# A hybrid decoder step: the query and the outer products of a sample step issued back to back, with one accumulator bank per head

## The chip, the cores and the metric

The kernel runs on one core of one Trainium2 chip. The metric is device time in microseconds for one execution. Three executions of the kernel before took 2542.88, 2548.21 and 2549.33 us (median 2548.21). One more execution was profiled; the rows below and in the prediction come from it.

## The reference, cut to what matters

One layer of a decoder is computed for a prompt of 512 tokens and for a batch of 8 decoding sequences of 4 tokens each (32 sample tokens), width 2048. A wide input projection gives queries, keys, values and gates of an mLSTM branch (4 heads of 512) and of a sliding-window attention branch (32 query heads, 4 key heads), and the gates of a merge; two projections, a merge, an output projection and a layer norm follow. The change lies in the mLSTM branch of the sample tokens. There each head of each sequence has a stored state, a 512 x 512 matrix C:

```python
num = jnp.einsum('bhts,bhsd->bhtd', s, v) + inter[..., None] * jnp.einsum('bhtk,bhkv->bhtv', q, C)
...
C_new = decay[..., None, None] * C + jnp.einsum('bhsk,bhsv->bhkv', w[..., None] * k, v)
```

For the samples there is one chunk of 4 tokens, so each of the 32 matrices (8 sequences x 4 heads, 1 MB each) is read once, queried (`q C`), updated by an outer product of keys and values, and written back.

## The kernel before, in words

**Input projection.** The core's time is mostly matmuls of split operands: a weight tile `raw` (128 x 1024) is cast to `wh` by ScalarE (line 198) and the rest `wl` is subtracted by VectorE (line 199), and three products are accumulated. In the stage of interest (`paired`, line 643) two column blocks of the weights form a pair, and seven *products* (`half_product`, line 602) make a pair. A product is 24 matmuls of 272 columns (16 at line 610, 8 at line 612) into a PSUM tile `bank`; a pair has three banks: products 0 and 3 write the first, 1 and 5 the second, 2, 4 and 6 the third. After each product `gather` (line 614) reads the bank, on ScalarE after products 0, 1 and 3 and on VectorE after 2, 4, 5 and 6 (lines 631, 635, 637, 639); after product 1 GpSimd also adds a piece (line 629). There are 72 pairs. The buffers of `bank` come from a pool of four in turn, so that one is spare.

**Work beside it.** Everything else of this stage is written as generators. After each product `tick` lets every live generator run to its next `yield`, so a `yield` is the distance of one product on TensorE. The order on TensorE is the order in which the code is written (`manual_schedule` for TensorE alone); the other engines' queues, SyncE's DMA queue among them, are ordered by a scheduler. `high_priority` pulls splits and gathers forward.

**Sample heads.** After the attention of the prompt and of the samples, `samples` (line 1131) runs `sample_head` (line 1068) for the four heads in turn. A head starts with `sample_prep`: small loads (`qs`, `ks`, `vs`, the normaliser), two yields, then a GpSimd copy `rep` of the keys into four parts (`four_parts`, line 972), two yields, and TensorE's products and transposes of it (lines 1000, 1001, 1005), and so on. Then come 8 *steps* (`s` = 0, 1: four of the eight sequences; `c` = 0 to 3: 128 of the 512 rows of C). Per step:

- the tile `ct` holds four blocks of C (1 MB, one load, two buffers); `qz` holds the queries, zero outside the sequence's own tokens (GpSimd memset and four copies, lines 1088 and 1091, two buffers);
- four yields; at the first the previous step's updated C is stored (`store`, two DMAs of 512 KB), at the third the next block is loaded (`load_C`), whose buffer must have been stored;
- the *query*: four matmuls with 32 output columns of the array each, side by side (line 1101), into a PSUM tile `sm`; ScalarE copies the result out (line 1105 or 1108) and GpSimd adds it to a sum in SBUF (line 1109, `r["sum"]`, which holds the buffer named `rep`);
- one yield;
- the *outer products*: four matmuls with 32 rows of the array each (line 1114) into four `sm` tiles, which VectorE folds into `ct` (line 1117, four of 128 x 512).

After the 8 steps `sample_finish` scales the sum, waits until the output gates of the head are computed (`gated`), and finishes the head. `sm` has four banks.

Of the kernel before, what the change touches and what calls it, by code (L numbers as in the profile page):

```python
# [15 lines left out]
F32 = mybir.dt.float32  # L16
F32R = mybir.dt.float32r
AF = mybir.ActivationFunctionType
ALU = mybir.AluOpType
# [60 lines left out]
def _build(tc, nc, i, o, es):  # L80
    PSUM = bass.MemoryType.PSUM
    ALL = slice(0, 128)

    def pool(stack, name, bufs, space=None, side=None):
        kw = {"space": space} if space is not None else {}
        if space is None:
            kw["side"] = side or "right"
            kw["reuse_waits"] = "tile"
        return stack.enter_context(tc.tile_pool(name=name, bufs=bufs, **kw))

    y_p, y_s, C_p, n_p, m_p, kb_p, vb_p, C_s, n_s, m_s, kb_s, vb_s = o
    V, A, G, PE = nc.vector, nc.scalar, nc.gpsimd, nc.tensor
# [7 lines left out]
    esP, psA = es.enter_context(ExitStack()), {}  # L100

    def open_psum(pairs):

        esP.close()
        psA["mm"] = pool(esP, "psP" if pairs else "psA", 4 if pairs else 2, PSUM)

    open_psum(False)
    dr = pool(es, "dr", 1, bass.MemoryType.DRAM)
# [3 lines left out]
    def nm(s):  # L112
        count[0] += 1
        return f"{s}_{count[0]}"

    def sm():
        return psB.tile([128, 512], F32, tag="sm", name=nm("sm"))
# [4 lines left out]
    def r32(ap):  # L122
        return ap.bitcast(F32)
# [830 lines left out]
    def st1(shape, tag, dt=F32, p="s1p"):  # L954
        return sp[p].tile(shape, dt, tag=tag, name=nm(tag))

    def w512():
        return sp["sw"].tile([128, 512], F32, tag="w", name=nm("w"))
# [10 lines left out]
    def four_parts(src):  # L969

        rep = st1([128, 4, 128], "rep")
        G.tensor_copy(by_part(rep[:]), src[:].rearrange("p c (b t) -> p (c b) t", t=NTS).unsqueeze(2)
                      .to_broadcast([128, 4 * NB, 4, NTS]))
        return rep
# [8 lines left out]
    def sample_prep(h, r):  # L983
        qs = st1([128, 4, NS], "qs", p="sw")
        ks_, vs = (st1([128, 4, NS], t_) for t_ in ("ks", "vs"))
        hc = slice(h * 4, h * 4 + 4)
        for t_, d_ in ((qs, d_q), (ks_, d_k), (vs, d_v)):
            nc.sync.dma_start(t_[:], d_[hc, :, SEQ:T].rearrange("c p t -> p c t"))
        nh_ = w512()
        nh = nh_[:8]  # L990
        nc.sync.dma_start(nh, i["state_mlstm_n"][:, h, :])
        yield
        yield
        rep = four_parts(ks_)
        yield
        yield

        pS, pb = sm(), sm()
        for c in range(4):
            PE.matmul(pS[:, 0:NS], rep[:, c], qs[:, c], start=(c == 0), stop=(c == 3))  # L1000
        PE.matmul(pb[:, 0:NS], cc[0:4, C_ID + h:C_ID + h + 1].to_broadcast([4, 128]), nM[:, SEQ:T],
                  start=True, stop=True)
        pk = sm()
        for c in range(4):
            PE.transpose(pk[:, c * 128:c * 128 + 128], rep[:, c], ident)
        ds, dl = st1([128, NS], "ds"), st1([128, NS], "dl")
        V.tensor_tensor(out=dl[:], in0=pb[:, 0:NS], in1=cc[:, C_SM:C_SM + NS], op=ALU.add)
        A.activation(dl[:], dl[:], AF.Exp, bias=colT1[:, 4, 0, h:h + 1])
        V.tensor_tensor(out=ds[:], in0=pS[:, 0:NS], in1=dl[:], op=ALU.mult)
        V.scalar_tensor_tensor(dl[:], pS[:, 0:NS], cc[:, C_R + 10:C_R + 11], dl[:], op0=ALU.mult, op1=ALU.mult)  # L1010
        Ph, Pst = st1([128, NS], "Ph", F32R), st1([128, NS], "Pst", F32R)
        A.copy(Ph[:], ds[:])
        V.scalar_tensor_tensor(Pst[:], r32(Ph[:]), cc[:, C_R + 11:C_R + 12], dl[:], op0=ALU.mult, op1=ALU.add)

        kA = st1([128, 512], "kA", F32R)
        rows_of_parts(kA, st1([128, 512], "Ab", F32R), pk, C_R + 11, (colW[:, 0, h:h + 1], colW[:, 1, h:h + 1]))
        repv = four_parts(vs)
        yield
        yield

        pvv = sm()
        for c in range(4):
            PE.transpose(pvv[:, c * 128:c * 128 + 128], repv[:, c], ident)
        V4 = st1([128, 512], "V4", F32R)
        rows_of_parts(V4, st1([128, 512], "Ab", F32R), pvv, C_R + 13, (1.0, cc[:, C_R + 12:C_R + 13]))

        pn = sm()
        for c in range(4):
            PE.transpose(pn[:, c * 8:c * 8 + 8], nh[:, c * 128:c * 128 + 128], ident[:8, :8])
        nT = st1([128, 4, NB], "nT")  # L1030
        V.tensor_copy(nT[:].rearrange("p c b -> p (c b)"), pn[:, 0:32])
        yield
        pq = sm()
        for c in range(4):
            PE.matmul(pq[:NS, 0:NB], qs[:, c], nT[:, c], start=(c == 0), stop=(c == 3))
        pd = sm()
        PE.matmul(pd[:NS, 0:2], Pst[:], ones_r[:], start=True, stop=True)
        pnn = sm()
        PE.matmul(pnn[:8, :], m8r[:], kA[:], start=True, stop=True)
        den = st1([32, 16], "den", p="sw")  # L1040
        V.scalar_tensor_tensor(den[:, 0:8], pq[:NS, 0:NB], colT2[0:32, 4, 1, h:h + 1], cc[0:32, C_M8:C_M8 + 8],
                               op0=ALU.mult, op1=ALU.mult, accum_out=den[:, 8:9])
        V.tensor_tensor(out=den[:, 9:10], in0=pd[:NS, 0:1], in1=den[:, 8:9], op=ALU.add)
        V.scalar_tensor_tensor(nh, nh, dcc[:, h:h + 1], pnn[:8, :], op0=ALU.mult, op1=ALU.add)
        nc.sync.dma_start(n_s[:, h, :], nh)
        r.update(kA=kA, V4=V4, Pst=Pst, den=den, qs=qs)
# [21 lines left out]
    def sample_head(h):  # L1068
        r = {}
        nxt = load_C(h, 0, 0)  # L1070
        yield from sample_prep(h, r)
        stores = []

        def store():

            with tc.issue_after(state["load"].ins):
                for dst, src in stores:
                    nc.sync.dma_start(dst, src)
            stores.clear()

        for s in range(2):
            Ab = st1([128, 512], "Ab", F32R)
            G.tensor_scalar(Ab[:], r32(r["kA"][:]), cc[:, C_R + 8 + s:C_R + 9 + s], None, op0=ALU.mult)
            for c in range(4):
                ct, more = nxt, (s, c) != (1, 3)

                qz = st1([128, 4, NS], "qz", p="sw")
                G.memset(qz[:], 0.0)
                for b in range(4):
                    t = (b * 2 + s) * NTS  # L1090
                    G.tensor_copy(qz[:, b, t:t + NTS], r["qs"][:, c, t:t + NTS])
                for j in range(4):
                    yield
                    if j == 0:
                        store()
                    elif j == 2 and more:
                        with tc.issue_after(state["load"].ins):
                            nxt = load_C(h, s + (c == 3), (c + 1) % 4)
                pC = sm()
                for b in range(4):  # L1100
                    PE.matmul(pC[b * 32:b * 32 + 32, :], qz[:, b], ct[:, b], start=True, stop=True,  # L1101
                              tile_position=(0, b * 32))
                if (s, c) == (0, 0):
                    r["sum"] = st1([128, 512], "rep")
                    A.copy(r["sum"][:], pC[:])
                else:
                    some = w512()
                    A.copy(some[:], pC[:])
                    G.tensor_tensor(out=r["sum"][:], in0=r["sum"][:], in1=some[:], op=ALU.add)
                yield  # L1110
                pus = [sm() for _ in range(4)]
                for b in range(4):
                    rows = slice(b * 32, b * 32 + 32)
                    PE.matmul(pus[b][:], Ab[rows, c * 128:c * 128 + 128], r["V4"][rows], start=True, stop=True,  # L1114
                              tile_position=(b * 32, 0))
                for b in range(4):
                    V.scalar_tensor_tensor(ct[:, b], ct[:, b], dcb[:, h, b * 2 + s:b * 2 + s + 1], pus[b][:],
                                           op0=ALU.mult, op1=ALU.add)
                    if b % 2:
                        stores.append((C_s[s + b * 2 - 2:s + b * 2 + 1:2, h, c * 128:c * 128 + 128, :].rearrange("b p v -> p b v"),  # L1120
                                       ct[:, b - 1:b + 1]))
        yield
        store()
        while h not in gated:
            yield
        yield from sample_finish(h, r)
# [458 lines left out]
    for g in range(G3):  # L1585
        ct = 16 - G3 + g
# [48 lines left out]
```

## Time and profile before

| | |
|---|---|
| three runs | 2542.88, 2548.21, 2549.33 us |
| profiled execution, its time | 2543.75 us |
| its span (first to last instruction) | 2541.9 us |
| TensorE matmul busy | 2509.8 us (99%) |
| VectorE, ScalarE, GpSimd busy | 1709.8, 1195.5, 377.4 us |
| mean granted TensorE clock | 0.994 |
| sample steps on TensorE | from 1085.4 to 1762.8 us |

In the timeline a row is a run of instructions of one line: start, time from the first to the last end, engine, line, operation, output and inputs, the tile of the array used (rows*columns) and the shape, how many. A matmul's own duration (some 290 ns) is longer than its distance to the next (about 125 ns), since matmuls overlap; the distance between starts is what counts. The four matmuls of a query appear as 8 records.

### The profile page before, as it was taken

The numbers are of one execution on the slowest core, as the hardware profiler recorded it, in microseconds if no ns is written. First come the engines' busy times: TensorE is split into PE (matmuls) and PEld (weight loads), VectorE is DVE, ScalarE is ACT, GpSimd is POOL, SyncE is SP. The second block draws the span as 40 slices with busy tenths as digits, with TensorE's granted clock in tenths as the row PEclk, the third lists the DMA queues.
The fourth block names the chain that finished last, engine by engine and source line by source line (L and its number), as shares of the span: only waits on it lengthen the run. The fifth ranks groups of instructions, "written<-read, shape, count | busy, mean of one in ns | idle before, by whom it ended". The sixth has DMA issues, their size and how long they took to land.

```text
span 2541.9 us, 48994 instructions
## 1 busy us (share of the span) xinstructions
PE 2509.8 (99%) x19995; PEld 2443.5 (96%) x19995; DVE 1709.8 (67%) x2506; ACT 1195.5 (47%) x1945; POOL 377.4 (15%) x434
## 2 busy tenths in 40 slices
PE   8999999999999999999999999999999999999997
PEld 7999999999999999999999999999999999999997
DVE  7867677777777777678787788777765653333236
ACT  4447667667667665443434544544533332222221
POOL 2111121111211211132022133121000000000002
PEclk9999999999999999999999999999999999999999
DMA  6566666666666654477577477477654555446332
GB/s 193 136 166 154 161 148 159 153 150 163 147 157 156 151 149 117 108 213 244 154 225 236 137 234 223 139 234 232 216 177 163 168 175 158 132 132 192 109 94 86
DMA packets 537105, 421.89 MB, mean 166 GB/s; under 512 B 43536, under 2 KB 449344, under 8 KB 536592
## 3 DMA queue, kind: packets, MB, share of 16 engines
q1 hardware_dynamic: 526800, 382.05, 50.8%
q0 software_dynamic: 10080, 36.70, 7.9%
q8 instruction: 157, 2.57, 0.4%
q14 instruction: 68, 0.56, 0.1%
HBM read 297.67 MB, written 86.42 MB: 151 GB/s over the span
## 4 chain that ended last, share of the span: by engine, by line
PE 57%; DVE 1%; issue 0%; POOL 0%; DVEq 0%
PE mm L207 21%; PE bank L610 18%; PE bank L612 9%; PE sm L1298 2%; PE sm L1101 1%; PE sm L1330 1%; PE sm L1343 1%; PE sm L207 1%; PE sm L1114 1%; DVE z L1537 0%; PE sm L1277 0%; PE sm L1285 0%; PE sm L1353 0%; DVE z L1542 0%; PE sm L1480 0%
## 5 line engine op out<-in xcount | busy, mean ns | idle before, releaser
L198 ACT CAST wh<-raw 128x1024 fp32r<-128x1024 f32 x604 | 632.3, 1048 | 918.9 <-PE bank L610 505.5
L199 DVE TENSOR_TENSOR wl<-raw,wh 128x1024 fp32r<-128x1024 f32 x604 | 756.5, 1254 | 360.5 <-ACT wh L198 353.1
L610 PE MATMUL bank<-xk,wh 128*128 128x272 f32 x2304 | 318.3, 291 | 0.0
L610 PEld LDWEIGHTS bank<-xk,wh 128*128 128x128 f32 x2304 | 299.5, 189 | 10.0 <-ACT wh L198 7.5
L590 DVE TENSOR_TENSOR raw<-raw,raw 128x1024 f32<-128x1024 f32 x218 | 278.4, 1278 | 6.3 <-DMA raw<-in_w_in 3.4
L207 PE MATMUL mm<-bh,wl 128*128 128x272 f32 x1024 | 214.4, 289 | 0.0
L207 PE MATMUL mm<-bh,wh 128*128 128x272 f32 x1024 | 214.2, 290 | 0.0
L207 PE MATMUL mm<-bl,wh 128*128 128x272 f32 x1024 | 213.4, 288 | 0.0
L612 PE MATMUL bank<-xk,wl 128*128 128x272 f32 x1152 | 167.5, 288 | 0.0
L629 POOL TENSOR_TENSOR ev<-p,ev 128x272 f32<-128x272 f32 x72 | 102.3, 1421 | 428.8 <-ACT ev L628 410.7
L207 PEld LDWEIGHTS mm<-bh,wh 128*128 128x128 f32 x1024 | 160.5, 188 | 2.3 <-issue 2.3
L207 PEld LDWEIGHTS mm<-bl,wh 128*128 128x128 f32 x1024 | 161.8, 188 | 0.0
L207 PEld LDWEIGHTS mm<-bh,wl 128*128 128x128 f32 x1024 | 160.6, 188 | 0.0
L612 PEld LDWEIGHTS bank<-xk,wl 128*128 128x128 f32 x1152 | 154.1, 189 | 0.0
L610 PE MATMUL bank<-n2h,wh 128*128 128x272 f32 x576 | 148.9, 291 | 2.0 <-ACT wh L198 2.0
L610 PE MATMUL bank<-a11h,wh 128*128 128x272 f32 x576 | 149.3, 291 | 0.0
L610 PE MATMUL bank<-s1h,wh 128*128 128x272 f32 x576 | 149.1, 292 | 0.1
L610 PE MATMUL bank<-s4h,wh 128*128 128x272 f32 x576 | 149.0, 292 | 0.0
L610 PE MATMUL bank<-n3h,wh 128*128 128x272 f32 x576 | 148.1, 290 | 0.0
L610 PE MATMUL bank<-a11l,wh 128*128 128x272 f32 x576 | 147.9, 289 | 0.0
L610 PE MATMUL bank<-n2l,wh 128*128 128x272 f32 x576 | 147.3, 288 | 0.0
L610 PE MATMUL bank<-n3l,wh 128*128 128x272 f32 x576 | 146.8, 287 | 0.0
(435 smaller groups left out, 5475.4 us busy)
## 6 DMA issues: line engine op xcount, KB each, us to landing
raw<-in_w_in SPq DMA_DIRECT2D x296, 512.0 KB
raw<-raw POOLq DMA_DIRECT2D x70, 512.0 KB, 4.9
C<-in_state_mlstm_C SPq DMA_DIRECT2D x32, 1024.0 KB
out<-C SPq DMA_DIRECT2D x64, 512.0 KB
raw<-in_w_proj_a SPq DMA_DIRECT2D x32, 512.0 KB
raw<-in_w_proj_m SPq DMA_DIRECT2D x32, 512.0 KB
raw<-in_w_out SPq DMA_DIRECT2D x32, 512.0 KB
d_sgm<-ev SPq DMA_DIRECT2D x16, 272.0 KB
```

Source lines behind the costliest of these rows:

```text
L198: A.copy(wh[:], raw[:])
L199: V.tensor_tensor(out=wl[:], in0=raw[:], in1=r32(wh[:]), op=ALU.subtract)
L207: PE.matmul(ps[:, f, :w], a[:, kk], b(k, c, w), start=(k == 0 and n == 0), stop=(k == 15 and n == 2))
L590: V.tensor_tensor(out=w[out][:], in0=w[a][:], in1=w[b][:], op=ALU.add)
L610: PE.matmul(ps, wh[:, k], x(p, k), start=(first and k == 0 and p == 0), stop=False, skip_group_check=True)
L612: PE.matmul(ps, wl[:, k], x(0, k), start=False, stop=(k == 7), skip_group_check=True)
L629: G.tensor_tensor(out=c22, in0=p1, in1=c11, op=ALU.subtract)
L1101: PE.matmul(pC[b * 32:b * 32 + 32, :], qz[:, b], ct[:, b], start=True, stop=True, tile_position=(0, b * 32))
L1114: PE.matmul(pus[b][:], Ab[rows, c * 128:c * 128 + 128], r["V4"][rows], start=True, stop=True, tile_position=(b * 32, 0))
L1298: PE.matmul(pp[:, 0:258], a[:, b * 128:b * 128 + 128], b_[:, b, f], start=(b == 0 and n == 0), stop=(b == 3 and n == 2))
L1330: PE.matmul(pp[:, 0:n], x_[c][:, b * 128:b * 128 + 128], y_[c][:, b * 128:SEQ], start=(c == 0 and m == 0), stop=(c == 3 and m == 2))
L1343: PE.matmul(pp[:, 0:258], x_[:, off:off + 128], y_[:, b, f], start=(b == 0 and n == 0), stop=(b == j and n == 2))
```

## The change

```diff
 def open_psum(pairs):
-    psA["mm"] = pool(esP, "psP" if pairs else "psA", 4 if pairs else 2, PSUM)
+    psA["mm"] = pool(esP, "psP" if pairs else "psA", 3 if pairs else 2, PSUM)
+    if pairs:
+        psA["sum"] = pool(esP, "psS", 1, PSUM)
...
 # sample_prep, after the loads
-        yield
-        yield
+        for _ in range(2 if h else 4):
+            yield
         rep = four_parts(ks_)
...
 # sample_head, in a step, after its four yields
-                pC = sm()
+                if (s, c) == (0, 0):
+                    pC = r["sum"] = psA["sum"].tile([128, 512], F32, tag="sum", name=nm("sum"))
                 for b in range(4):
-                    PE.matmul(pC[b * 32:b * 32 + 32, :], qz[:, b], ct[:, b], start=True, stop=True,
+                    PE.matmul(pC[b * 32:b * 32 + 32, :], qz[:, b], ct[:, b], start=(s, c) == (0, 0), stop=not more,
                               tile_position=(0, b * 32))
-                if (s, c) == (0, 0):
-                    r["sum"] = st1([128, 512], "rep")
-                    A.copy(r["sum"][:], pC[:])
-                else:
-                    some = w512()
-                    A.copy(some[:], pC[:])
-                    G.tensor_tensor(out=r["sum"][:], in0=r["sum"][:], in1=some[:], op=ALU.add)
-                yield
                 pus = [sm() for _ in range(4)]
```

The queries of a head are summed in one PSUM bank over all 8 steps; ScalarE's copy and GpSimd's addition of each step go. The yield between query and outer products goes, so a step is four yields long and not five. The bank comes from the pairs' pool, which has three buffers instead of four during the whole paired stage. The first head waits two products longer before `rep`. In the changed kernel the line numbers are up to 5 off: products are lines 612 and 614, the query 1104, the outer products 1109, `rep` 974, its users 1002 to 1007.

On TensorE, the third step of the first head before: the query (line 1101, C block and `qz` into `sm`), a whole product of the pairs (16 rows at line 610 and two at 612), and the outer products. First the query:

```order
L610 MATMUL bank_13216<-s4l_1010,wh_13296 128x272
L612 MATMUL bank_13216<-s4h_1009,wl_13297 128x272 x8
L1101 MATMUL sm_13393<-C_13169,qz_13257 32x512 x4
L610 MATMUL bank_13268<-xk_5_112,wh_13329 128x272
L610 MATMUL bank_13268<-xk_7_114,wh_13329 128x272
```

The next product of the pair follows the query. At its end come the outer products, from the same C block's step:

```order
L612 MATMUL bank_13268<-xk_5_112,wl_13330 128x272 x4
L612 MATMUL bank_13268<-xk_6_113,wl_13330 128x272 x4
L1114 MATMUL sm_13438<-V_1703_12810,Ab_12866 128x512
L1114 MATMUL sm_13439<-V_1703_12810,Ab_12866 128x512
L1114 MATMUL sm_13440<-V_1703_12810,Ab_12866 128x512
L1114 MATMUL sm_13441<-V_1703_12810,Ab_12866 128x512
L610 MATMUL bank_13461<-a11h_108,wh_13364 128x272
```

Here a new pair begins behind them. The same step on TensorE in the changed kernel:

```order
L614 MATMUL bank_13209<-s4h_1009,wl_13294 128x272 x8
L1104 MATMUL sum_13079<-C_13202,qz_13254 32x512 x4
L1109 MATMUL sm_13394<-V_1709_12879,Ab_12938 128x512
L1109 MATMUL sm_13395<-V_1709_12879,Ab_12938 128x512
L1109 MATMUL sm_13396<-V_1709_12879,Ab_12938 128x512
L1109 MATMUL sm_13397<-V_1709_12879,Ab_12938 128x512
L612 MATMUL bank_13265<-xk_5_112,wh_13326 128x272
```

The product that stood between the query and the outer products now stands behind both, and the query writes `sum`.

On TensorE, where the first head's preparation uses `rep`, before (products of the pairs around it; `n2h`, `n3h`, `s4h`, `xk` are the activations of products 2, 4, 5 and 3 or 6):

```order
L612 MATMUL bank_12683<-n2h_121,wl_12612 128x272 x8
L1000 MATMUL sm_12709<-qs_12565,rep_12642 128x32 x4
L1001 MATMUL sm_12710<-nM,cc 128x32
L1005 MATMUL sm_12716<-cc,rep_12642 128x128 x4
L610 MATMUL bank_12615<-xk_5_112,wh_12644 128x272
```

The group follows product 2 of a pair. And in the changed kernel:

```order
L614 MATMUL bank_12684<-n3h_123,wl_12680 128x272 x8
L1002 MATMUL sm_12778<-qs_12568,rep_12710 128x32 x4
L1003 MATMUL sm_12779<-nM,cc 128x32
L1007 MATMUL sm_12785<-cc,rep_12710 128x128 x4
L612 MATMUL bank_12650<-s4h_1009,wh_12712 128x272
```

The group moved from behind product 2 to behind product 4 of the same pair, two products later.

On GpSimd, from the last gather before `rep` on, in the kernel before:

```order
L629 TENSOR_TENSOR ev_12675<-p_1673_12640,ev_12674 128x272
L1091 COPY qz_12868<-qs_12565 128x4 x4
L1091 COPY qz_13062<-qs_12565 128x4 x2
L972 COPY rep_12642<-ks_12566 128x512
L1091 COPY qz_13062<-qs_12565 128x4 x2
```

Six `qz` copies stand ahead of `rep`, two behind it. And in the changed kernel:

```order
L631 TENSOR_TENSOR ev_12676<-p_1673_12643,ev_12675 128x272
L1093 COPY qz_12940<-qs_12568 128x4 x4
L1093 COPY qz_13096<-qs_12568 128x4 x2
L974 COPY rep_12710<-ks_12569 128x512
L1093 COPY qz_13096<-qs_12568 128x4 x2
```

The queue stands as it did here: `rep` keeps its place behind six of the `qz` copies. What GpSimd loses are the 28 additions of later rows (line 1109).

## The prediction, made before the changed kernel ran

> **What bounds the kernel now.** I read the page first, then what TensorE waits for from the first sample head to the end of the pairs, then TensorE's timeline through a step, and last the windows that compare the four heads.
>
> ```profile
> span 2541.9 us, 48994 instructions
> PE 2509.8 (99%) x19995; PEld 2443.5 (96%) x19995; DVE 1709.8 (67%) x2506; ACT 1195.5 (47%) x1945; POOL 377.4 (15%) x434
> PE mm L207 21%; PE bank L610 18%; PE bank L612 9%; PE sm L1298 2%; PE sm L1101 1%; PE sm L1330 1%; PE sm L1343 1%; PE sm L207 1%; PE sm L1114 1%; DVE z L1537 0%; PE sm L1277 0%; PE sm L1285 0%; PE sm L1353 0%; DVE z L1542 0%; PE sm L1480 0%
> ```
>
> TensorE is busy 99% of the span and the chain that ended last is made of its lines. The answer on TensorE's waits between 1050 and 1804 us has a single row:
>
> ```profile
> PE sm L1000 <- POOL rep L972: 2.4, 1, 2.4
> ```
>
> So in the whole stretch of the sample heads TensorE waited once, at the start of the first head. Time can be won only from that wait, or by making TensorE's own stream shorter. Copies, additions and waits of other engines are worth nothing in themselves.
>
> **Query and outer products together.** No matmul is added or removed. What changes is how often the stream passes between the whole array and a part of it. Here are the last product before a query, the query, the product behind it, the outer products, and the start of the next product:
>
> ```profile
> 1115.05 1.16 PE L612 MATMUL bank<-n3h,wl 128*128 128x272 f32 x8
> 1116.05 0.29 PE L610 MATMUL bank<-s4h,wh 128*128 128x272 f32 x1
> ...
> 1118.05 1.17 PE L612 MATMUL bank<-s4h,wl 128*128 128x272 f32 x8
> 1119.14 1.07 PE L1101 MATMUL sm<-C,qz 128*32 128x512 f32 x8
> 1120.14 2.29 PE L610 MATMUL bank<-xk,wh 128*128 128x272 f32 x16
> 1122.27 1.16 PE L612 MATMUL bank<-xk,wl 128*128 128x272 f32 x8
> 1123.35 0.51 PE L1114 MATMUL sm<-V,Ab 32*128 32x512 f32 x4
> 1123.79 0.39 PE L610 MATMUL bank<-a11h,wh 128*128 128x272 f32 x1
> 1124.01 0.29 PE L610 MATMUL bank<-a11l,wh 128*128 128x272 f32 x1
> ```
>
> Undisturbed, 8 matmuls of line 612 take 1.00 (1115.05 to 1116.05) and a product 3.00 us (1115.05 to 1118.05). Counted by starts, the query begins 0.09 late (1118.05 + 1.00 against 1119.14) and takes 1.00 to the next product's start. The product behind it takes 3.21 (1120.14 to 1123.35) instead of 3.00: 16 matmuls take 2.13 instead of 2.00 and the last 8 take 1.08 instead of 1.00. The outer products take 0.44, and the first matmul behind them 0.22 instead of 0.125, 0.10 more. A step thus costs 1.09 + 0.21 + 0.44 + 0.10 = 1.84 us beside its five products.
>
> In the change no product stands between the two, so the 0.21 of that product, 0.13 on entry and 0.08 on exit, has no place. What is not shown is the passage from the query straight to the outer products. If it is like the one from the query to a whole-array product, the query takes its 1.00 as before and the outer products their 0.44 with 0.10 behind: 1.63 per step, 0.21 less. The nearest row for a query-like group that is followed by something other than a whole-array product is the end of a head:
>
> ```profile
> 1772.42 1.05 PE L1056 MATMUL sm<-w,cc 128*32 128x512 f32 x2
> 1773.39 0.42 PE L1057 MATMUL sm<-V,Pst 128*32 128x512 f32 x1
> ```
>
> There the same 512 columns take 0.97 to the next matmul, whose part of the array is the same, against 1.00 with eight records in front of the whole array. What follows hardly matters, so I take 0.21, and over 32 steps 6.7 us. The ends: the passage also costs the 0.21 again (no gain), or the outer products' stretch shrinks by about as much again, their weights being loaded under the query (0.40 a step, 12.8 us).
>
> The Trainium skill, "TensorEngine Tiling (Array Packing)", section Tiling Modes, says that a change of the tiling mode, not of the tile alone, drains the array. 128*32 and 32*128 are different modes, so by that rule one passage stays between them and one of four goes, which speaks for 6.7 and against 12.8; no row of this trace has the two next to each other.
>
> **The first head's two extra yields.** The one wait costs more than its 2.4 us:
>
> ```profile
> 1054.24 1.17 PE L612 MATMUL bank<-n2h,wl 128*128 128x272 f32 x8
> 1057.78 1.39 PE L1000 MATMUL sm<-qs,rep 128*128 128x32 f32 x8 [2.37 <-POOL rep L972]
> ...
> 1078.36 1.16 PE L612 MATMUL bank<-a11h,wl 128*128 128x272 f32 x8
> ...
> 1245.00 1.17 PE L612 MATMUL bank<-s1h,wl 128*128 128x272 f32 x8
> ...
> 1263.44 1.16 PE L612 MATMUL bank<-xk,wl 128*128 128x272 f32 x8
> ...
> 1058.40:1065.20 6.80, 6.80 (x32) 6.67 (x32) 1.55 (x5) 2.40 (x5) 0.61 (x1) 0.50 0.45 109
> 1244.00:1249.00 5.00, 5.00 (x43) 4.92 (x42) 3.27 (x4) 2.47 (x4) 1.45 (x1) 1.00 0.28 82
> ```
>
> The first two rows bracket the first head's group; the third is five products later: 1078.36 - 1054.24 = 24.12 us. The next two rows are the same places of the second head: 18.44 us. The difference is 5.7 us. The windows (the number before the DMA share is the granted clock) show why: right behind the wait TensorE ran at half its clock for 6.8 us, which costs 3.4, and the second head's group, without a wait, ran at 1.00. Is the wait gone? GpSimd made `rep` here:
>
> ```profile
> 1054.33 2.86 POOL L1091 COPY qz<-qs 128x4 f32<-128x4 f32 x6
> 1057.12 0.61 POOL L972 COPY rep<-ks 128x512 f32<-128x512 f32 x1
> ```
>
> Its queue keeps that order and its loads are issued as before, so `rep` is done at 1057.73. TensorE, ready at 1057.78 - 2.37 = 1055.4, now arrives two products later, 1061.4: 3.7 us to spare. I take the whole 5.7 us.
>
> **Three banks instead of four.** The new pair's product 1 now needs the bank of product 5 and its product 2 that of product 6, each two products (6.0 us) after these end. The latest reading of that kind:
>
> ```profile
> 1546.59 1.16 PE L612 MATMUL bank<-xk,wl 128*128 128x272 f32 x8
> 1549.59 1.17 PE L612 MATMUL bank<-a11h,wl 128*128 128x272 f32 x8
> 1550.72 0.43 DVE L639 SCALAR_TENSOR_TENSOR ev<-bank,p 128x272 f32<-128x272 f32 x1
> 1553.59 0.29 PE L610 MATMUL bank<-n2h,wh 128*128 128x272 f32 x1
> ```
>
> Product 6 ends at 1547.8, VectorE reads its bank up to 1551.15, and product 2 of the next pair starts at 1553.59: 2.4 us to spare at the worst. Within a pair, product 4 waits for the gather of product 2 across one product only, and not even that makes a wait row. I cost it at 0; if the cover goes, each late gather costs its excess.
>
> **Removed copies and additions, and a denser schedule.** They are these:
>
> ```profile
> L1109 POOL TENSOR_TENSOR rep<-rep,w 128x512 f32<-128x512 f32 x28 | 40.7, 1454 | 14.0 <-ACT w L1108 14.0
> L1108 ACT COPY w<-sm 128x512 f32<-128x512 f32 x28 | 16.4, 587 | 18.4 <-PE sm L1101 18.3
> L1117 DVE SCALAR_TENSOR_TENSOR C<-C,dcb,sm 128x512 f32<-128x512 f32 x128 | 86.9, 739 | 0.0
> 1270.00:1395.00 125.00, 125.00 (x980) 113.97 (x980) 98.86 (x108) 49.46 (x62) 33.01 (x55) 1.00 0.74 230
> SPq L962 <- DMA out<-C: 52.3, 23, 4.8
> 1115.07 1.09 SPq L962 DMA_DIRECT2D C<-in_state_mlstm_C  x1
> ```
>
> ScalarE is freed of 16 and GpSimd of 41 us, both far from busy (49 and 33 of 125 us): nothing on the path. But a step shrinks from 5 x 3.00 + 1.84 = 16.84 to 4 x 3.00 + 1.63 = 13.63 us, and carries the same loads. VectorE's four updates are 4 x 0.74 = 2.96 us a step; in the window there are 125 / 16.84 = 7.42 steps, so the rest is 98.86 - 22.0 = 76.9 us, 2.07 per product, and its share goes from 79% to (4 x 2.07 + 2.96) / 13.63 = 82%. C moves 2.10 MB a step: 125 GB/s before, 154 after, 29 more than the window's 230, so the DMA share goes from 0.74 to about 0.83. The load issued at 1115.07 serves the query 20.9 us later (1135.98 = 1119.14 + 16.84); now it has one product and 0.2 us less, 17.7. A megabyte at half of 230 GB/s is an estimated 9 us. SyncE's queue still holds its load of C until the store has landed (up to 4.8 us), with weight loads behind it; between store and load stand two products, as before. I cost all this at 0. The samples end some 100 us earlier (32 x 3.21), which frees nothing on TensorE.
>
> **Sum.** -6.7 - 5.7 = -12.4 us. The profiled execution took 2543.75 us, 4.5 below the median of the runs; from the one this gives 2531.4, from the other 2535.8. I say 2534, and work out the rivals from the middle of the two, 2546.0.
>
> **Rivals.**
>
> *The wait stays, or another takes its place* at the first head: `rep` 3.7 us later than before, or the value copy behind it. 2546.0 - 6.7 = 2539. For it: GpSimd's copies hang on DMAs that just landed. Against: the queue order is unchanged.
>
> *The passage from query to outer products costs as much as the two that it replaces.* 2546.0 - 5.7 = 2540. The change would then not do what it says. Against it: the row of 0.97.
>
> *The half clock belongs to the small matmuls of the head's preparation, not to the wait.* Then only 2.3 us of the 5.7 go: 2546.0 - 6.7 - 2.3 = 2537. Against it: the second head's group at 1.00. The Trainium skill, "TensorE: Matmul & The Clock Gate", section What's actually happening, speaks for this one: it wants about 3.4 us of idleness, a whole window, before the clock is halved, and here 2.37 us and a few small matmuls were enough.
>
> *Both passages vanish:* 2546.0 - 12.8 - 5.7 = 2527.5.
>
> *C comes late,* the rival on the slower side. The first step behind which TensorE would wait is any with a load that lands over 17.7 us after its issue. With 0.39 us a step (12.4 / 32) the gain is gone, and with over 0.62 the kernel is slower by more than 7.6; at 1.2 us a step it takes 2546.0 - 12.4 + 38.4 = 2572. For it: a share of 0.83, in which queues grow faster than the load. Against it: no query waited for C so far.
>
> **How the numbers follow.** What a measurement of this kernel can tell from no change is about 0.3%, 7.6 us. Forecast 0.60, half clock 0.06, both passages 0.07: faster by more than that, 0.73. The wait stays 0.10 and the passages cost the same 0.08: within it, 0.18. C late, or VectorE behind it, 0.09: slower. The range runs from the case at 2527.5, less 2.5, to that at 2540, with the scatter of the runs (5): 2525 to 2545. It leaves out the slower rival.
>
> **What would show it.** In the changed profile the wait row at `rep` is gone, and no granted clock under 1.00 stands between 1050 and 1804; steps lie 13.6 us apart; the outer products start 1.00 behind the query; no row has TensorE wait for a gather on VectorE or for C; the sample steps end near 1660. I would be wrong with a half clock elsewhere, or with weights that come late in the denser stretch.

## The result, and the profile after

The changed kernel took 2534.76 us (median of 5 runs, 2529.57 to 2537.36) against 2548.21 before (2542.88 to 2549.33): a ratio of 0.9951, 95% interval 0.9938 to 0.9964, or 13.4 us less. In its own profiled execution, of 2535.28 us, the page begins so:

```profile
span 2533.5 us, 48923 instructions
PE 2504.9 (99%) x19995; PEld 2442.9 (96%) x19995; DVE 1701.5 (67%) x2506; ACT 1174.8 (46%) x1911; POOL 326.0 (13%) x406
```

TensorE is still busy 99%, with the same number of matmuls; ScalarE lost 34 instructions, GpSimd 28. The answer on TensorE's waits between 1050 and 1804 us has no row left. TensorE's timeline through a step (start, time, line; the query is now line 1104, the outer products 1109):

```profile
1115.27 1.17 PE L614 MATMUL bank<-s4h,wl 128*128 128x272 f32 x8
1116.37 1.06 PE L1104 MATMUL sum<-C,qz 128*32 128x512 f32 x8
1117.37 0.51 PE L1109 MATMUL sm<-V,Ab 32*128 32x512 f32 x4
1117.81 2.28 PE L612 MATMUL bank<-xk,wh 128*128 128x272 f32 x16
...
1130.02 1.07 PE L1104 MATMUL sum<-C,qz 128*32 128x512 f32 x8
```

The outer products start 1.00 behind the query, just where a product started before, and take 0.44. Steps are 13.65 us apart. TensorE's timeline at the first head's preparation:

```profile
1063.55 1.16 PE L614 MATMUL bank<-n3h,wl 128*128 128x272 f32 x8
1064.55 0.97 PE L1002 MATMUL sm<-qs,rep 128*128 128x32 f32 x8
...
1081.98 1.17 PE L614 MATMUL bank<-n2h,wl 128*128 128x272 f32 x8
```

And the window around it (the granted clock is the number before the DMA share):

```profile
1060.00:1080.00 20.00, 20.00 (x167) 19.52 (x166) 15.59 (x26) 13.15 (x18) 6.47 (x8) 1.00 0.48 126
```

From the product ahead of it to the fifth behind it are now 18.43 us, as at the second head (18.44), where it had been 24.12. The clock stays whole. The keys' copy on GpSimd comes in time:

```profile
1060.43 0.61 POOL L974 COPY rep<-ks 128x512 f32<-128x512 f32 x1
```

It ends at 1061.04, and TensorE uses it at 1064.55: 3.5 us to spare, where 3.7 had been worked out. The other engines in the steps of the second head, from the windows:

```profile
1248.00:1357.00 109.00, 109.00 (x858) 98.10 (x857) 89.13 (x102) 38.63 (x46) 15.64 (x45) 1.00 0.84 261
```

And from the waits of SyncE's queue, the load of C behind the stores:

```profile
SPq L964 <- DMA out<-C: 92.0, 24, 7.0
```

VectorE is busy 82% and the DMA share is 0.84 at 261 GB/s (0.74 and 230 before); the stores hold the queue for 92 us in all instead of 52.

**The two profiles differ by less than the medians,** by 8.4 us instead of 13.4. Part of that is the clock elsewhere. Ahead of the sample heads, in the sample attention, whose code is the same:

```profile
1000.00:1056.00 56.00, 55.41 (x439) 51.77 (x437) 33.56 (x47) 20.09 (x31) 7.96 (x11) 0.97 0.37 95
```

That was before. The same window after:

```profile
1000.00:1056.00 56.00, 56.00 (x422) 52.37 (x422) 30.35 (x44) 18.69 (x29) 4.87 (x5) 0.91 0.31 81
```

The mean granted clock over these 56 us was 0.97 and 0.91. At half clock for the missing share that is 2 x 0.03 x 56 = 3.4 and 10 us of half clock, so after lost some 3.4 us more there in this one execution. With it the rows account for the 8.4: 32 x 0.19 = 6.1 us in the steps and 5.7 at the first head, less 3.4. A single span of this kernel is therefore read to about 5 us; the verdicts below rest on several runs, and on the rows that the clock does not touch.

### The profile page after: what moved, and what is told of

Its sections match the earlier page's. It is cut to its first block, busy times and chain, and to the rows that moved or that the text cites. A ratio compares the mean times of both kernels' runs of the same rounds, so it can differ in the third digit from the quotient of the medians.

```text
span 2533.5 us, 48923 instructions
## 1 busy us (share of the span) xinstructions
PE 2504.9 (99%) x19995; PEld 2442.9 (96%) x19995; DVE 1701.5 (67%) x2506; ACT 1174.8 (46%) x1911; POOL 326.0 (13%) x406
## 4 chain that ended last, share of the span: by engine, by line
PE 93%; DVE 2%; DMA 1%; issue 1%; ACT 0%; DVEq 0%; ACTq 0%
PE bank L612 39%; PE mm L209 21%; PE bank L614 19%; PE sm L1293 2%; PE sum L1104 1%; PE sm L1325 1%; PE sm L1338 1%; PE sm L718 1%; PE sm L758 1%; PE sm L748 1%; PE sm L209 1%; DMA raw<-in_w_in 1%; PE sm L1109 1%; DVE z L1532 0%; PE sm L917 0%
## 5 line engine op out<-in xcount | busy, mean ns | idle before, releaser
L201 DVE TENSOR_TENSOR wl<-raw,wh 128x1024 fp32r<-128x1024 f32 x604 | 748.5, 1241 | 353.0 <-ACT wh L200 346.4
```

Of the source, the lines that this page charges most:

```text
L201: V.tensor_tensor(out=wl[:], in0=raw[:], in1=r32(wh[:]), op=ALU.subtract)
```

## The experiments

The theory: each step is 0.2 us shorter because one passage between the whole array and a part of it goes, and the first head loses a wait with the half clock behind it. Rivals: the copies and additions that went; the denser schedule; the wait alone.

| kernel | against before, 95% interval | at the whole clock, us (estimate) |
|---|---|---|
| before | 1 | 2527.4 |
| the change | 0.9951 (0.9938 to 0.9964) | 2517.5 |
| the change once more | 0.9956 (0.9942 to 0.9970) | 2520.1 |
| the change, old yields at the first head | 0.9974 (0.9963 to 0.9986) | 2522.2 |
| before, with the two extra yields alone | 0.9968 (0.9955 to 0.9981) | 2526.8 |
| the change, query and outer products apart | 0.9989 (0.9978 to 1.0001) | 2526.3 |
| before, with three banks | 1.0002 (0.9993 to 1.0012) | 2527.3 |
| the change, outer products in two halves | 1.0034 (1.0021 to 1.0046) | 2538.7 |
| the change, copies and additions kept | 0.9945 (0.9927 to 0.9964) | 2520.6 |
| the change, sample attention spread | 0.9954 (0.9939 to 0.9968) | 2522.8 |
| the change, five yields a step | 0.9956 (0.9939 to 0.9973) | 2519.6 |
| five yields and attention spread | 0.9955 (0.9939 to 0.9971) | 2523.2 |
| the change, outer products first | 0.9962 (0.9944 to 0.9980) | 2521.2 |

The last column needs a word. The kernel before ran 64 more times beside the experiments, and its time goes with the mean granted clock of the run: those at 0.991 or less took 2549.5 us or more, those at 0.995 or more 2545.1 or less. In these traces the clock is either whole or half, so a span times its mean clock estimates what the span would be at the whole clock. The column is the mean of that over a kernel's runs, good to about 1 us (2 us where a kernel has few runs). The sixteen runs of the change are 8 us below the kernel before in it. The rows have 6.1 us in the steps and the first head's wait itself, 2.4, which makes 8.5. The rest of the 13.4 us between the medians is clock and scatter.

**One part each.** First the change without its two extra yields:

```diff
-        for _ in range(2 if h else 4):
+        for _ in range(2):
             yield
```

> The change without the first head's two extra yields: query and outer products together, three banks, a bank of its own for the sum. Theory (each step is 0.21 us shorter because one passage between the whole array and a part of it goes; the first head's wait is a separate 5.7 us): 6.7 us faster than before, -0.26%, with the wait of some 2.4 us at the first head's copy of the keys back and the granted clock at one half behind it. Rival (the gain is the first head's wait alone): no change, within 0.1%. Rival (freed ScalarE and GpSimd, and the denser steps, bring the gain): all of the 13.4 us, -0.5%, wait or not.

Measured: 0.26% faster, as the theory has it; both rivals' numbers, none and 0.5%, lie outside the interval. At the whole clock, where the wait's half clock does not count, it is 5.2 us. The steps are the new ones, and TensorE's wait is back:

```profile
PE sm L1002 <- POOL rep L974: 2.4, 1, 2.4
```

So is the half clock, in the window behind it:

```profile
1064.60:1071.40 6.80, 6.80 (x31) 6.67 (x31) 1.55 (x5) 2.51 (x5) 0.61 (x1) 0.50 0.46 108
```

Then the two yields alone, in the kernel before:

```diff
-        yield
-        yield
+        for _ in range(2 if h else 4):
+            yield
         rep = four_parts(ks_)
```

> The kernel before with only the two extra yields of the first head. Theory: the one wait row between 1050 and 1804 us goes, and with it the half clock behind it: 5.7 us faster, -0.22%; steps stay 16.84 us apart. Rival (the half clock belongs to the small matmuls of the preparation, as the section What's actually happening of the Trainium skill's page TensorE: Matmul & The Clock Gate would have it, since the wait is under 3.4 us): 2.3 us faster, -0.09%, with a granted clock of one half still standing near 1060 us. Rival (the wait moves to the next thing that GpSimd makes): no change.

Measured: 0.32% faster; the interval holds the theory's 0.22% and neither 0.09% nor none. No wait row is left between 1050 and 1804 us, and the window around the preparation has the whole clock:

```profile
1055.00:1080.00 25.00, 25.00 (x207) 24.52 (x206) 18.45 (x23) 16.04 (x23) 9.91 (x13) 1.00 0.60 154
```

The small matmuls of the preparation are all still in that window, so they do not bring the half clock alone: it came with the wait, in all three profiles that have it (before, the kernel above, and the three-bank kernel below). The Trainium skill, "TensorE: Matmul & The Clock Gate", section What's actually happening, asks for some 3.4 us of idleness. Here 2.4 us with small matmuls behind them were enough. The column at the whole clock, 0.6 us below the kernel before from five runs, is too coarse to show the 2.4.

**Everything but the togetherness:**

```diff
+                yield
                 pus = [sm() for _ in range(4)]
```

> The change with the yield between query and outer products put back: queries still summed in their own bank, no copies and additions, three banks, four yields at the first head, but a product stands between query and outer products again. Theory: only the first head's 5.7 us stay, -0.22%; the step is 16.84 us again and the product between the two takes 3.21 us. Rival (copies and additions were the cost): 13 us faster, as with the whole change.

Measured: 0.11% faster, 2.8 us, with an interval that just reaches the 0.22% of the theory and excludes the rival's 0.5%. TensorE's timeline shows the old step:

```profile
1121.02 1.07 PE L1104 MATMUL sum<-C,qz 128*32 128x512 f32 x8
1124.13 1.16 PE L614 MATMUL bank<-s1h,wl 128*128 128x272 f32 x8
1125.22 0.51 PE L1110 MATMUL sm<-V,Ab 32*128 32x512 f32 x4
```

Query to outer products are 4.20 us again, against 4.21 in the prediction's rows (1119.14 to 1123.35). Without copies and additions, a step with a product in between costs what it cost. This kernel gained a third of what the yields alone did. At the whole clock the two are 0.5 us apart, so the difference lies in the granted clock of the runs, 0.994 in the mean here and 0.996 there; why it differs is not shown.

**Three banks in the kernel before:**

```diff
-        psA["mm"] = pool(esP, "psP" if pairs else "psA", 4 if pairs else 2, PSUM)
+        psA["mm"] = pool(esP, "psP" if pairs else "psA", 3 if pairs else 2, PSUM)
```

> The kernel before with three banks for the pairs instead of four, nothing else (one bank stays unused). Theory: 0, within 0.1%, no row in which TensorE waits for a gather on VectorE. Rival (the spare bank hides late gathers): slower by some us, with TensorE waiting for lines 637 or 639.

Measured: 1.0002. But a wait for a gather on VectorE there is, at 135 us, near the start of the paired stage: product 6 waits for the gather of product 4 (line 635). First this kernel, then the one with the yields alone, which has four banks:

```profile
PE bank L610 <- DVE ev L635: 2.0, 1, 2.0
PE bank L610 <- DVE ev L635: 1.8, 1, 1.8
```

So it does not come from the missing bank: within a pair, products 4 and 6 write the same bank however many the pool has. No such wait is in the sample steps; the only rows of TensorE's waits from 150 us to the end of the pairs are these, of which the second is in the sample attention:

```profile
PE sm L1000 <- POOL rep L972: 2.4, 1, 2.4
PE sm L869 <- ACT kT L854: 0.2, 1, 0.2
```

**The price of a trip.** The outer products cut in two, so that the array is left once more per step:

```diff
                 for b in range(4):
+                    if b == 2:
+                        yield
                     rows = slice(b * 32, b * 32 + 32)
```

> The change with the outer products cut in two: two matmuls behind the query, a yield, then the other two behind the next product. Theory (a trip from the whole array to a part and back costs about 0.6 us however little it carries: before, the outer products alone cost 0.08 + 0.44 + 0.10): every step is 0.6 us longer than in the change (16.65 us with five products), 20 us over 32 steps, so 6 us slower than the kernel before, +0.25%. Rival (the price goes with the matmuls, not with the trips): the same as the change, -0.5%.

Measured: 1.0034, 0.34% slower than before (the theory's 0.25% is inside). The expected step of 16.65 us was an addition gone wrong: 13.65 + 3.00 + 0.6 is 17.25, and TensorE's timeline has that:

```profile
1121.06 1.07 PE L1104 MATMUL sum<-C,qz 128*32 128x512 f32 x8
1122.05 0.50 PE L1111 MATMUL sm<-V,Ab 32*128 32x512 f32 x2
...
1138.30 1.06 PE L1104 MATMUL sum<-C,qz 128*32 128x512 f32 x8
1139.29 0.50 PE L1111 MATMUL sm<-V,Ab 32*128 32x512 f32 x2
1139.72 2.28 PE L612 MATMUL bank<-xk,wh 128*128 128x272 f32 x16
```

Steps are 17.24 us apart, so the second trip costs 17.24 - 13.65 - 3.00 = 0.59 us. Two matmuls take 0.43 us where four took 0.44, and that is most of it. The groups of instructions (count, busy time, mean ns of one) show why, first in the change, then in this kernel:

```profile
L1109 PE MATMUL sm<-V,Ab 32*128 32x512 f32 x128 | 16.2, 495 | 0.0
L1111 PE MATMUL sm<-V,Ab 32*128 32x512 f32 x128 | 32.0, 495 | 0.0
```

A matmul lasts 495 ns in both; in the change four run side by side, here two, so TensorE is busy with the same 128 for twice as long. The passages themselves are left with 0.59 - 0.43 = 0.16 us, close to the 0.19 that a step of the change saves. So the rival is out, but the 0.6 of the theory is not the price of passing alone.

**Copies and additions kept, the rest as in the change:**

```diff
-                if (s, c) == (0, 0):
-                    pC = r["sum"] = psA["sum"].tile([128, 512], F32, tag="sum", name=nm("sum"))
+                pC = psA["sum"].tile([128, 512], F32, tag="sum", name=nm("sum"))
                 for b in range(4):
-                    PE.matmul(pC[b * 32:b * 32 + 32, :], qz[:, b], ct[:, b], start=(s, c) == (0, 0), stop=not more,
+                    PE.matmul(pC[b * 32:b * 32 + 32, :], qz[:, b], ct[:, b], start=True, stop=True,
                               tile_position=(0, b * 32))
+                if (s, c) == (0, 0):
+                    r["sum"] = st1([128, 512], "rep")
+                    A.copy(r["sum"][:], pC[:])
+                else:
+                    some = w512()
+                    A.copy(some[:], pC[:])
+                    G.tensor_tensor(out=r["sum"][:], in0=r["sum"][:], in1=some[:], op=ALU.add)
                 pus = [sm() for _ in range(4)]
```

> The change with ScalarE's copy and GpSimd's addition of each step kept: the bank of its own takes one step's query at a time, the sum is in SBUF as before; query and outer products stay together. Theory: the copies are off the path, so it is as fast as the change, -0.5% against before, with steps of 13.65 us. Rival (the freed engines brought part of it): half of the gain or less, with waits of TensorE for the bank.

Measured: 0.9945, all of the gain. The 28 additions are back, in the groups of instructions:

```profile
L1111 POOL TENSOR_TENSOR rep<-rep,w 128x512 f32<-128x512 f32 x28 | 36.9, 1318 | 9.4 <-ACT w L1110 9.4
```

They are off the path, for TensorE's steps are those of the change:

```profile
1111.27 1.06 PE L1103 MATMUL sum<-C,qz 128*32 128x512 f32 x8
1112.27 0.51 PE L1115 MATMUL sm<-V,Ab 32*128 32x512 f32 x4
...
1124.92 1.07 PE L1103 MATMUL sum<-C,qz 128*32 128x512 f32 x8
```

**The change once more,** for the scatter and a second profile.

> The changed kernel once more, on the same chip as the others. Theory: -0.5% against before, steps 13.65 us apart, no wait between 1050 and 1804 us; the span minus half of the half-clock time is the same as in its first profile (2525.0 us) within 2 us, while the half-clock time itself differs.

Measured: 0.9956, its steps 13.65 us apart. But this execution's span was 2542.2 us at a mean clock of 0.992, the first one's 2533.5 at 0.994. At the whole clock that is 2522 against 2518: some 3.5 us apart and not within 2 (the 2525.0 of the expectation takes off less half clock than 0.994 makes). There are waits that the first profile did not have. One is 1.4 us for a gather at 135 us, as in the three-bank kernel. TensorE's waits name the other:

```profile
PE bank L614 <- DVE wl L201: 2.3, 1, 2.3
```

It is at 1201 us. VectorE's timeline ahead of it:

```profile
1190.97 1.40 DVE L1112 SCALAR_TENSOR_TENSOR C<-C,dcb,sm 128x512 f32<-128x512 f32 x2
1196.14 1.23 DVE L592 TENSOR_TENSOR raw<-raw,raw 128x1024 f32<-128x1024 f32 x1 [3.77 <-DMA raw<-in_w_in]
```

And SyncE's queue:

```profile
1188.20 0.38 SPq L964 DMA_DIRECT2D C<-in_state_mlstm_C  x1
1189.85 4.17 SPq L583 DMA_DIRECT2D raw<-in_w_in  x1
1194.11 4.99 SPq L1080 DMA_DIRECT2D out<-C  x2
```

At the end of the first head VectorE sat 3.77 us for a weight load, the split behind it came late, and TensorE waited 2.3 us. From the last query of this head to the first of the next are 68.09 us, where the first profile has 64.09. The issues of SyncE at that place took 4.17 and 4.99 us, where one of line 583 takes 0.38 as a rule (144 of them, 0.37 to 5.63 in the first profile; up to 5.47 in the one of before, whose steps leave more time).

**Sample attention spread,** to see the half clocks of the windows at 1000 us:

```diff
                 yield
                 yield
+            else:
+                yield
             PT = PTs[b % 2]
```

> The change with one more yield in the sample attention, ahead of the sample heads: the small matmuls of lines 917 and 918 come in eight blocks of some 1.9 us with a product between them, instead of four blocks of 3.8 us. Theory (a block of small matmuls that fills a whole stretch of 3.4 us brings the half clock, as the wait at the first head did): no granted clock under 1.00 between 1000 and 1050 us; in the profiles so far 3.4 to 13.6 us of half clock stood there, 1.7 to 6.8 us lost, so some 3 us faster than the change even after four more trips: -0.6% against before. Rival (these half clocks come by chance, wherever they fall): as the change, -0.5%, half clocks of the same length somewhere.

Measured: 0.9954, no better than the change; the interval reaches the theory's 0.6% and holds the rival's 0.5%, so the time does not decide between them. The windows show that the clock did what was expected, in this kernel and in its sibling below, against 0.91 and 0.82 in the two profiles of the change. This kernel:

```profile
1000.00:1056.00 56.00, 56.00 (x452) 52.11 (x451) 33.88 (x45) 19.39 (x30) 5.91 (x6) 1.00 0.30 79
```

The change, in its second profile:

```profile
1000.00:1056.00 56.00, 56.00 (x387) 52.17 (x386) 28.99 (x42) 15.48 (x24) 3.08 (x4) 0.82 0.25 63
```

But the kernel with copies kept, whose blocks are the long ones, had a clock of 1.00 there too, so long blocks do not bring the half clock every time. The expected 3 us do not show in the time. One reason stands in TensorE's waits, again a late split at a head's end, with a half clock of 3.4 us behind it:

```profile
PE bank L614 <- DVE wl L201: 1.9, 1, 1.9
```

What spreading does show is steadier runs. All eleven runs of this kernel and its sibling have a mean clock of 0.995 or more and lie between 2533.2 and 2536.6 us. Of the change's sixteen, six have that clock, and they lie between 2529.4 and 2544.0. At the whole clock the two spread kernels are some 3.5 us longer than their counterparts, which eats the gain; no run here says where all of that comes from.

**Five yields a step,** query and outer products together but C at the old pace, and the same with the attention spread:

```diff
-                for j in range(4):
+                for j in range(5):
                     yield
```

> The change with five yields in front of the query instead of four: query and outer products stay together, but a step takes five products again (16.63 us) and C moves at the old pace. Theory (the passage saves 0.21 us a step at any pace; in two of five profiles of dense steps a weight load came late behind the stores of C, a wait of 1.9 to 2.3 us and a half clock behind it): the steps' gain stays, no row in which TensorE waits for line 201 between 1050 and 1804 us, a DMA share of some 0.75 in the steps; as fast as the change or 2 us faster, -0.5 to -0.6%. Rival (the gain comes from the denser schedule): half of it is lost.

> Five yields per step and the spread sample attention in one kernel. Theory: no wait and no half clock between 1000 and 1804 us, some 4 us faster than the change, -0.65% against before. Rival (half clocks and late loads come by chance elsewhere): as the change, -0.5%.

Measured: 0.9956 and 0.9955. Half of the gain, 0.25%, lies just outside both intervals. So the steps' gain does not come from the density, and undoing the density gains nothing that can be measured. The first of them still shows a late split, of 0.4 us, the second has none in the sample steps; the DMA share in the steps is back at 0.74 and 0.76. The second had a clock of 1.00 from 1000 to 1804 us, as expected, but waited 1.5 us at the end of the pairs, for a gather. Neither beats the change.

**Outer products first:** the query's matmuls stand behind those of the outer products.

> The change with the order turned round: outer products first, the query behind them. Theory (one passage between two parts of the array, either way): the same stretch of 1.63 us, steps of 13.65 us, -0.5% against before. Rival (the query's two passes hide the loading of the outer products' weights, and nothing hides the query's): steps some 0.1 us longer, 3 us in all.

Measured: 0.9962, and on TensorE the same stretch with its parts exchanged:

```profile
1113.98 0.50 PE L1104 MATMUL sm<-V,Ab 32*128 32x512 f32 x4
1114.42 1.07 PE L1109 MATMUL sum<-C,qz 128*32 128x512 f32 x8
1115.41 2.29 PE L612 MATMUL bank<-xk,wh 128*128 128x272 f32 x16
```

0.44 to the query and 0.99 to the product, 1.43 in all against 1.44 in the change (1.00 and 0.44): the order does not matter.

## Why the prediction was right, and where it was not

**The passage** (0.21 us a step, 6.7 in all) was sized right. Steps went from 16.84 to 13.65 us, a product and 0.19, which makes 6.1. The value taken for the unknown passage, that what follows the query hardly matters, is what the rows show: 1.00 to the outer products, 1.00 to a product. The row that it was taken from (0.97) stays within one part of the array, so that it holds for a change of part was an assumption that came true. The outer bound (0.40) fell with it: the outer products still take 0.44. The first kernel of the experiments, which is the change without the two yields, gained 0.26%, 6.6 us, and since three banks, copies and density are worth nothing that the runs can tell, the togetherness is what is left. The Trainium skill, "TensorEngine Tiling (Array Packing)", section Tiling Modes, says that a change of the tiling mode drains the array. No run here shows a drain as such; the runs show the price, 0.2 us for the passage saved, the same between two parts in either order.

**The first head's wait** (5.7 us) was right in its rows: 24.12 became 18.43, 5.69 us. The rival of the half clock that stays fell. In the times of the runs the 5.7 is less sharp: the two extra yields alone gained 0.32% (0.19 to 0.45), everything but the togetherness 0.11% (up to 0.22), because the clock elsewhere moves each run by several us.

**Three banks, copies and additions** (0): the ratios 1.0002 and 0.9945 say so. That no row would have TensorE wait for a gather on VectorE held in the first profile of the change and failed in the second, at 135 us, by a wait that four banks have too.

**The denser schedule** was the step that was mis-sized. VectorE's 82% and the DMA share of 0.83 came out as worked (82%, 0.84), and C was never late. What I had cost at 0 is the weight load behind the stores of C in SyncE's queue: of six profiles with dense steps (the change twice, old yields, copies kept, attention spread, outer products first) three have TensorE wait for a split at a head's end, 2.3, 1.9 and 1.0 us, the longer two with a half clock of 3.4 us behind them. Of the seven profiles with five products a step one has such a wait, of 0.4 us. In an execution that has it, it costs up to 4 us, a third of the gain. I had named the mechanism and looked for it at C, where the slack was 17.7 us, though weights that come late stood among the signs of being wrong. That the density makes these waits is likely from the counts and not shown: undoing it did not change the time. The forecast that no half clock would stand between 1050 and 1804 us held in the first profile and failed in the second.

**The sum** (12.4) met 13.4 within the interval (9.2 to 15.8 us). That the median came within 1 us of the 2534 is luck: single runs of the change lie between 2529.4 and 2544.0, and the rows themselves have 6.1 + 5.7 = 11.8.

## What to carry to other kernels

When the matmul engine is full, look for what its stream pays at the borders between the whole array and parts of it. Here two small matmuls took as long as four side by side, and each trip paid some 0.2 us of passages on top, so small tiled groups belong together, whatever else is copied around them. A single wait on a busy TensorE can cost more than its length, because of the clock behind it; its price is the distance between the same two places at a head that did not wait. Before a schedule is made denser, check the loads that stand in the same queue behind the new traffic, not only the traffic itself.

## What the runs showed of the hardware that was not expected

Half clocks without any wait: during the sample attention, with blocks of small matmuls of some 3.7 us and no gap on TensorE, the granted clock over 56 us was between 0.82 and 1.00 from profile to profile (0.97 before, 0.91 and 0.82 in two of the change), and 1.00 in both profiles in which the blocks were halved. At 0.82 that is some 20 us at half clock. From the start of the product ahead of the first block to that of the twelfth product behind it, that profile has 61.48 us (1004.78 to 1066.26), the one with copies kept, at 1.00, has 52.66 (1003.79 to 1056.45): 8.8 us lost. The runs of the kernel before, 2540.3 to 2552.6 us, scatter by that much and with their mean clock; that the sample attention is where most of it is lost is likely, but only profiles show the place.

Nor does a wait bring the half clock every time. All thirteen profiles have a wait of 2.4 us near 43 us; nine have a half clock behind it (0.76 over the window 42 to 49), four have none. Four have a wait of 2.3 to 2.7 us near 57 us, all at 1.00 from 56 to 62.

SyncE's issue of a DMA, 0.38 us as a rule, took 4 to 5 us where loads and stores of C and weights met.
